# First gemm of the FFNs: products V and W2 accumulate onto the banks of X and W

## The chip, the cores and the metric

The kernel runs on one core of a Trainium2 chip. The metric is device time in microseconds (us) of one execution, taken as the median of three runs. PE is the matmul engine, DVE the vector engine, ACT the activation engine, POOL the GpSimd engine, SP the queue that issues DMAs.

## The reference

Two layers of a diffusion backbone work on 768 tokens (256 context, 512 latent) of width 1024. Each layer is FFN, token mixer, FFN; layer 0 mixes by differential attention, layer 1 by neighbourhood attention. The change is in the FFNs, of which there are four:

```python
def _ffn_sublayer(h, mod, g_pre, g_post, w_in, w_out):
    shift, scale, gate = mod
    u = _modulate(_rmsnorm(h, g_pre), shift, scale)
    a, b = jnp.split(u @ w_in, 2, axis=-1)
    y = (jax.nn.silu(a) * b) @ w_out
    return h + MACARON_W * gate * _rmsnorm(y, g_post)
```

Here `u @ w_in` (1024 by 2 x 2816) is the first gemm. Shift, scale and gate come from another product, of SiLU(c) with a table of adaLN weights.

## The kernel before

The four FFNs are named f00, f01, f10, f11 (layer, then first or second of the layer). Tokens are worked on as two sets of 384, in f11 as two sets of 256. The first gemm (`FirstGemm`) splits its weights into 11 column groups of 256 columns, numbered 0 to 10, once for the gate half (`a`, which goes through SiLU) and once for the other half (`b`, which is multiplied on): items run a0, b0, a1, ... b10, and the trace names what belongs to item a9 of f00 as f00a9. Raw weights and their splits carry the number of the item in the load order instead: f0025 is item a9, f0026 is b9.

Each item is a product of 2 x 2 blocks done by seven block products instead of eight, the scheme of Strassen and Winograd: `X` = A11 with the first set's upper half, `V` = A12 with its lower half, `Y`, `Z`, `W` and `W2` of sums of weight blocks (S1 and S2 in tile `s12`, S3 and S4 in tile `s34`) with sums of the inputs or the second set, `Z2` of block A22. The sums of weights are POOL's (L473 to L476). Each operand is kept as a high and a low part: ACT casts the high part (L126), DVE subtracts to get the low part (L127). In the trace these tiles end in h and l: a1h, a1l for A11 and A12; bh, bl for `s12`; ch, cl for `s34`; dh, dl for A22. One block product is then four slices of the inner dimension times three passes, so 12 matmuls (L132), and within each slice the third pass is the one that reads the low part of the weights.

Items are of two kinds. The kind is set by EARLY = (7, 7, 6, 5): for the first 7, 7, 6, 5 groups of f00, f01, f10, f11 the first two products were done earlier, and X comes back from memory as `p1`; these items (kind R) have five products, 60 matmuls, and the others (kind F) seven, 84 matmuls. So there are 50 R items and 38 F items.

PSUM is held by two pools: `psum_g` has two tiles of one bank, `psum_y` three tiles of two banks. X and Y are the two banks of one `psum_y` tile, Z and W of another; V, Z2 and W2 are tiles of `psum_g`. In the trace, an instruction on Y or W is named after its tile, X or Z.

DVE adds the products together: `u` = X + Y (L548, after ACT copied X at L561), c1 = u + Z, c1's second half = that + W, `u` = u + W, c1 += Z2, c0's second half = u + W2, and in F items c0's first half = V + `u`. Then ACT applies SiLU (a items) or DVE and POOL multiply (b items, L593 and L584), and the result `h` goes to memory. A second gemm reads it back; its first split of `h` (f00hl, f01hl) is made in the DVE queue while the first gemm runs.

Between the products `work.step` issues pieces of other work: in R items, while they last, the adaLN product (`mods_pairs`, tile `am`, L243), a group of four matmuls of 32 x 512 that write the four strips of 32 partitions of one `psum_g` tile, followed by a DVE add (`mb`, L247). There are 24 such groups in f00, 16 in f01, 24 in f10 and none in f11. The same form of matmul stands at the start of the kernel as `md` (L165). The trace has two records for each of these matmuls.

The program is written through a tile framework, which tracks dependencies by whole tile and chooses the order of instructions on each engine itself; the order of the code is only its input.

Of the kernel before, what the change touches and what calls it, by code (L numbers as in the profile page):

```python
# [12 lines left out]
AF = mybir.ActivationFunctionType  # L13
ALU = mybir.AluOpType
# [42 lines left out]
def kernel(  # L57
# [20 lines left out]
    nc = tc.nc  # L78
# [32 lines left out]
    def psum_g(name):  # L111
        return psg.tile([P, 512], F32, tag="g", name=name)

    def psum_y(name):
        return psy.tile([P, 2 * 512], F32, tag="y", name=name)
# [11 lines left out]
        eng.tensor_tensor(out=lo, in0=src, in1=hi.bitcast(F32), op=ALU.subtract)  # L127
        return hi, lo

    def mm3(ps, lhs, rhs, first=True, last=True):  # L130
        for n, (i, j) in enumerate(PASSES):
            nc.tensor.matmul(ps, lhsT=lhs[i], rhs=rhs[j], start=first and n == 0, stop=last and n == 2)  # L132

    svec = const.tile([P, 5 * KC], F32, name="svec")
    nc.sync.dma_start(svec, cvec)
# [231 lines left out]
    class Work:  # L367
# [3 lines left out]
        def add(self, g):  # L371
            self.gens.append(g)
# [45 lines left out]
    class FirstGemm:  # L418
# [82 lines left out]
            self.load(1)  # L501
            self.step(0)

        def prod(self, ps, a, b):
            for k in range(4):
                mm3(ps, [x[:, k, :] for x in a], [x[:, k, :] for x in b], k == 0, k == 3)

        def cols(self, t, k0):
            c = slice(t * P, t * P + self.n)
# [32 lines left out]
        def group(self, i, kind_, g, x, work):  # L542
            n, pool, nm = self.n, self.pool, f"{self.nm}{'ab'[x]}{g}"
            o = self.ops[i]
            S = [[y[:, q] for y in o[s]] for s in ("S12", "S34") for q in (0, 1)]
            T = [[y[:, q] for y in self.sums["T"]] for q in range(3)]
            nx = lambda m=1: self.step(i + 1, m)
            add = lambda out, a, b: nc.vector.tensor_tensor(out=out, in0=a, in1=b, op=ALU.add)  # L548
            if x == 0:
                self.sa = pool.tile([P, 2, 2 * n], F32, tag="sa", name=nm + "sa")  # L550
            sa = self.sa
            c = [sa[:, y, :] if x == 0 else pool.tile([P, 2 * n], F32, tag=f"c{y}", name=f"{nm}c{y}") for y in range(2)]
            u2 = pool.tile([P, n], F32, tag="u2", name=nm + "u")
            nx()
            XY = psum_y(nm + "X")
            X, Y = XY[:, 0:n], XY[:, 512 : 512 + n]
            if kind_ == "F":
                self.prod(X, [y[:, 0:4] for y in o["A1"]], self.cols(self.t1, 0))
            self.prod(Y, S[1], T[1])
            if kind_ == "F":  # L560
                nc.scalar.copy(u2, X)  # L561
                V = psum_g(nm + "V")[:, 0:n]
                self.prod(V, [y[:, 4:8] for y in o["A1"]], self.cols(self.t1, 4))
                add(c[0][:, 0:n], V, u2)
                add(u2, Y, u2)
            else:
                add(u2, Y, o["p1"])
            nx()
            ZW = psum_y(nm + "Z")
            Z, W = ZW[:, 0:n], ZW[:, 512 : 512 + n]  # L570
            self.prod(Z, S[2], T[2])
            self.prod(W, S[0], T[0])
            add(c[1][:, 0:n], u2, Z)
            add(c[1][:, n:], c[1][:, 0:n], W)
            add(u2, u2, W)
            nx()
            work.step(1)
            Z = psum_g(nm + "Z2")[:, 0:n]
            self.prod(Z, o["A22"], self.cols(self.t2, 0))
            add(c[1][:, 0:n], c[1][:, 0:n], Z)  # L580
            if x == 0:
                nc.scalar.activation(c[1], c[1], AF.Silu)
            else:
                nc.gpsimd.tensor_tensor(out=sa[:, 1, :], in0=sa[:, 1, :], in1=c[1], op=ALU.mult)  # L584
            W = psum_g(nm + "W2")[:, 0:n]
            self.prod(W, S[3], self.cols(self.t2, 4))
            nx(9)
            add(c[0][:, n:], u2, W)
            f0 = n if kind_ == "R" else 0
            if x == 0:  # L590
                nc.scalar.activation(sa[:, 0, f0:], c[0][:, f0:], AF.Silu)
            else:
                nc.vector.tensor_tensor(out=sa[:, 0, f0:], in0=sa[:, 0, f0:], in1=c[0][:, f0:], op=ALU.mult)  # L593
                c0 = self.t1 * P
                nc.sync.dma_start(hdr[self.slot][2 * g][:, c0 + f0 : c0 + 2 * n], sa[:, 0, f0:])
                nc.sync.dma_start(hdr[self.slot][2 * g + 1][:, c0 : c0 + 2 * n], sa[:, 1, :])
            work.step(1)
# [143 lines left out]
    def out_ahead(l, w_out, sets, done):  # L741
# [25 lines left out]
        for hf in range(2):  # L767
            c = slice(hf * 512, hf * 512 + 512)
            ws = [split(r[:, :, c], [P, 2, 512], f"{nm}w{hf}{q}") for q, r in enumerate(raws)]
            for i in range(len(tiles)):  # L770
                ps = psum_g(f"{nm}g{hf}{i}")
                for u in range(HELD):
                    w = [x[:, u % 2] for x in ws[u // 2]]
                    mm3(ps, [o[:, x, u, i * P : (i + 1) * P] for x in range(2)], w, u == 0, u == HELD - 1)
                    if u == HELD // 2 - 1:
                        yield 9
                nc.scalar.copy(part[:, i, c], ps)
                yield 9

    def outproj(pool, l, w_out, sets, nxt, more, ahead):  # L780
# [49 lines left out]
        def mm(ps, q, i, c, first, last):  # L830
            hh, w = ops[q]
            mm3(ps, [x[:, i * P : (i + 1) * P] for x in hh], [x[:, c] for x in w], first, last)
# [151 lines left out]
    def attend(nslot, qk, vs, scores, values, rate, pattern, prog, ahead, opening):  # L984
        def stream():
            v = iter(())
            for u in range(1, 8):
# [3 lines left out]
                for x in pattern:  # L991
                    src = v if x == "V" else g
                    if next(src, "end") != "end":
# [18 lines left out]

        first = {"q": qk(0, "q"), "k": qk(0, "k"), "V": vs(0)}
        for x in opening:
# [383 lines left out]
    with Main("m0") as mp:  # L1398
        first = FirstGemm(mp, 0, 0, full, "f00", lead=True)
# [16 lines left out]
        for x in SCRIPT.split():  # L1416
            if x[0] == "m":
                hf, m, n = (int(y) for y in x[1:])
# [116 lines left out]
```

## Time and profile before

| | |
|---|---|
| median of three runs | 2891.31 us (2886.37 to 2895.78) |
| the profiled execution | 2882.43 us, of which the span is 2880.0 us |
| mean granted PE clock | 0.988 |
| PE busy | 2755.4 us, 96% of the span, 15928 records |
| DVE busy | 1986.4 us, 69% |
| ACT, POOL busy | 1209.5 us (42%), 883.0 us (31%) |

The span is from the first to the last instruction of the profiled execution. Busy shares are means over stages of different kind, so each stage has to be read by itself.

### The profile page before, as it was taken

The page shows a single profiled execution, that of the slowest core. Times are in us where ns is not written, and L with a number is a line of the kernel's source. Part 1 is how long each engine was busy: PE and PEld are TensorE (multiplying, and loading weights), DVE is VectorE, ACT ScalarE, POOL GpSimd, SP SyncE. Part 2 cuts the span into 40 slices and gives each one's busy share as a digit, 9 for nine tenths or more (in the row PEclk, how much of TensorE's full clock was granted, in tenths as well). Part 3 has the DMA queues.
Part 4 walks back from the last instruction along what each step waited for, and adds up shares of the span by engine and source line. Part 5 has one row for each costly group of instructions (what it writes and reads, how often), then busy time and mean ns, then how long its engine had stood idle before and what let it go on. Part 6 is the DMA issues. An engine that isn't in the chain of part 4 may idle for free. (4 is left out here: it accounts for less than half of the span.)

```text
span 2880.0 us, 41455 instructions
## 1 busy us (share of the span) xinstructions
PE 2755.4 (96%) x15928; PEld 2441.6 (85%) x15928; DVE 1986.4 (69%) x2554; ACT 1209.5 (42%) x1894; POOL 883.0 (31%) x715
## 2 busy tenths in 40 slices
PE   7799999999999988999999999999999999889999
PEld 5788998888888778899988888998878888789987
DVE  5677664667777696777555867674654556799965
ACT  5322333435555553233343522233444446544444
POOL 2455420020000055554210455340122110377710
PEclk9999999999999999999999999999999999999999
DMA  8577346643343476853465577436644444654375
GB/s 279 189 278 273 103 147 218 213 123 86 105 118 88 140 240 199 285 172 104 171 210 193 178 271 266 162 107 219 217 160 118 118 118 130 222 167 147 125 252 192
DMA packets 304820, 511.55 MB, mean 178 GB/s; under 512 B 17456, under 2 KB 226224, under 8 KB 297456
## 3 DMA queue, kind: packets, MB, share of 16 engines
q1 hardware_dynamic: 304336, 508.26, 53.7%
q8 instruction: 125, 2.05, 0.3%
q14 instruction: 71, 0.58, 0.1%
q10 hardware_dynamic: 288, 0.66, 0.1%
HBM read 410.15 MB, written 63.05 MB: 164 GB/s over the span
## 5 line engine op out<-in xcount | busy, mean ns | idle before, releaser
L1243 POOL TENSOR_TENSOR bias<-bp,nneg 128x128 f32<-128x128 f32 x112 | 52.3, 505 | 190.1 <-issue 99.2
L127 DVE TENSOR_TENSOR f01hl<-f01h,f01hh 128x384 fp32r<-128x384 f32 x44 | 26.4, 599 | 74.7 <-ACT f01hh L126 74.6
L127 DVE TENSOR_TENSOR f00hl<-f00h,f00hh 128x384 fp32r<-128x384 f32 x44 | 26.5, 602 | 72.9 <-ACT f00hh L126 72.8
L127 DVE TENSOR_TENSOR f10hl<-f10h,f10hh 128x384 fp32r<-128x384 f32 x44 | 26.0, 591 | 67.7 <-ACT f10hh L126 67.6
L243 PE MATMUL am<-aw,s 128*32 128x512 f32 x512 | 68.3, 606 | 4.1 <-DVE f10b0c L548 3.0
L126 ACT CAST f10hh<-f10h 128x384 fp32r<-128x384 f32 x44 | 22.7, 516 | 113.6 <-PE f10y L721 93.9
L126 ACT CAST f01hh<-f01h 128x384 fp32r<-128x384 f32 x44 | 22.7, 516 | 109.8 <-PE f01y L721 95.1
L126 ACT CAST f00hh<-f00h 128x384 fp32r<-128x384 f32 x44 | 22.7, 516 | 107.2 <-PE f00y L721 92.7
L132 PE MATMUL av<-pt,davh 128*128 128x256 f32 x224 | 44.6, 292 | 0.0
L247 DVE TENSOR_TENSOR mb<-am,mb 128x512 f32<-128x512 f32 x64 | 43.7, 683 | 0.0
L1305 PE MATMUL nav<-npt,navh 128*64 128x256 f32 (+1 forms) x320 | 39.3, 365 | 0.0
L132 PEld LDWEIGHTS av<-pt,davh 128*128 128x128 f32 x224 | 36.4, 193 | 1.3 <-ACT pt L1165 0.2
L1305 PEld LDWEIGHTS nav<-npt,navh 128*64 128x64 f32 x320 | 22.0, 136 | 12.2 <-issue 1.9
L132 PE MATMUL av<-pt,davl 128*128 128x256 f32 x112 | 31.7, 283 | 0.0
L126 ACT CAST f11hh<-f11h 128x256 fp32r<-128x256 f32 x44 | 17.7, 406 | 33.1 <-DMA f11h<-hr 22.1
L127 DVE TENSOR_TENSOR f11hl<-f11h,f11hh 128x256 fp32r<-128x256 f32 x44 | 20.2, 464 | 13.4 <-ACT f11hh L126 13.4
L243 PEld LDWEIGHTS am<-aw,s 128*32 128x32 f32 x512 | 10.1, 108 | 20.4 <-issue 10.2
L282 POOL TENSOR_SCALAR f01y0r<-f01y0s 128x1 f32<-128x1 f32 x1 | 0.2, 192 | 84.5 <-ACT f01y0j L276 84.5
L282 POOL TENSOR_SCALAR f10y0r<-f10y0s 128x1 f32<-128x1 f32 x1 | 0.2, 192 | 84.5 <-ACT f10y0j L276 84.5
L282 POOL TENSOR_SCALAR f00y0r<-f00y0s 128x1 f32<-128x1 f32 x1 | 0.2, 192 | 84.5 <-ACT f00y0j L276 84.5
L282 POOL TENSOR_SCALAR f00y3r<-f00y3s 128x1 f32<-128x1 f32 x1 | 0.2, 193 | 79.3 <-ACT f00y3j L276 79.3
L282 POOL TENSOR_SCALAR f10y3r<-f10y3s 128x1 f32<-128x1 f32 x1 | 0.2, 192 | 79.3 <-ACT f10y3j L276 79.3
(9736 smaller groups left out, 11615.4 us busy)
## 6 DMA issues: line engine op xcount, KB each, us to landing
aw<-in_ada_w SPq DMA_DIRECT2D x63, 1024.0 KB
f00r<-in_ffn_w_in SPq DMA_DIRECT2D x22, 1024.0 KB
f01r<-in_ffn_w_in SPq DMA_DIRECT2D x22, 1024.0 KB
f10r<-in_ffn_w_in SPq DMA_DIRECT2D x22, 1024.0 KB
f11r<-in_ffn_w_in SPq DMA_DIRECT2D x22, 1024.0 KB
f00o<-in_ffn_w_out SPq DMA_DIRECT2D x21, 1024.0 KB
f01o<-in_ffn_w_out SPq DMA_DIRECT2D x21, 1024.0 KB
f10o<-in_ffn_w_out SPq DMA_DIRECT2D x21, 1024.0 KB
```

The source lines that it names most:

```text
L126: nc.scalar.copy(hi, src)
L127: eng.tensor_tensor(out=lo, in0=src, in1=hi.bitcast(F32), op=ALU.subtract)
L132: nc.tensor.matmul(ps, lhsT=lhs[i], rhs=rhs[j], start=first and n == 0, stop=last and n == 2)
L243: nc.tensor.matmul(ps[32 * c : 32 * c + 32], lhsT=s32[:, k], rhs=w[:, c // 2, c % 2 * 512 : c % 2 * 512 + 512], start=True, stop=True,)
L247: nc.vector.tensor_tensor(out=acc, in0=ps, in1=acc, op=ALU.add)
L282: nc.gpsimd.tensor_scalar(r, ss, 1.0, EPS, ALU.mult, ALU.add)
L1243: nc.gpsimd.tensor_tensor(out=bias[:, m, :].rearrange("p (a b) -> p a b", a=8), in0=view, in1=neg[:, m, :].rearrange("p (a b) -> p a b", a ...
L1305: nc.tensor.matmul(av[64 * i : 64 * i + 64, half * 256 + c0 : half * 256 + c0 + n], lhsT=made[u]["v"][0][:, key, vc : vc + 64], rhs=made[u ...
```

## The change

V is no longer a tile of its own. Once the copy of X has been taken, V's twelve matmuls accumulate onto X's bank (no start flag), so that the bank holds X + V, and SiLU (a items) or a new DVE multiply (`times`, b items) reads it from there. W2 accumulates likewise onto W's bank, after W has been added to c1, and the add of W to `u` goes away. The add c1 = Z + u moves in the code to between products Z and W. The copy of X moves to right behind X, and V to behind W. The multiply of the first row of halves is two instructions of 384 columns for an F item, where it was one of 768. So one DVE add goes from each R item and two from each F item; the count of matmuls stays. `skip_group_check` relaxes a check in the simulator and is no instruction.

```diff
@@ -127,9 +127,11 @@
         eng.tensor_tensor(out=lo, in0=src, in1=hi.bitcast(F32), op=ALU.subtract)
         return hi, lo
 
-    def mm3(ps, lhs, rhs, first=True, last=True):
+    def mm3(ps, lhs, rhs, first=True, last=True, onto=False):
         for n, (i, j) in enumerate(PASSES):
-            nc.tensor.matmul(ps, lhsT=lhs[i], rhs=rhs[j], start=first and n == 0, stop=last and n == 2)
+            nc.tensor.matmul(
+                ps, lhsT=lhs[i], rhs=rhs[j], start=first and n == 0, stop=last and n == 2, skip_group_check=onto
+            )
 
     svec = const.tile([P, 5 * KC], F32, name="svec")
     nc.sync.dma_start(svec, cvec)
@@ -501,9 +503,9 @@
             self.load(1)
             self.step(0)
 
-        def prod(self, ps, a, b):
+        def prod(self, ps, a, b, onto=False):
             for k in range(4):
-                mm3(ps, [x[:, k, :] for x in a], [x[:, k, :] for x in b], k == 0, k == 3)
+                mm3(ps, [x[:, k, :] for x in a], [x[:, k, :] for x in b], k == 0 and not onto, k == 3, onto)
 
         def cols(self, t, k0):
             c = slice(t * P, t * P + self.n)
@@ -551,46 +553,45 @@
             sa = self.sa
             c = [sa[:, y, :] if x == 0 else pool.tile([P, 2 * n], F32, tag=f"c{y}", name=f"{nm}c{y}") for y in range(2)]
             u2 = pool.tile([P, n], F32, tag="u2", name=nm + "u")
+            times = lambda out, y: nc.vector.tensor_tensor(out=out, in0=y, in1=out, op=ALU.mult)
             nx()
             XY = psum_y(nm + "X")
             X, Y = XY[:, 0:n], XY[:, 512 : 512 + n]
             if kind_ == "F":
                 self.prod(X, [y[:, 0:4] for y in o["A1"]], self.cols(self.t1, 0))
+                nc.scalar.copy(u2, X)
             self.prod(Y, S[1], T[1])
-            if kind_ == "F":
-                nc.scalar.copy(u2, X)
-                V = psum_g(nm + "V")[:, 0:n]
-                self.prod(V, [y[:, 4:8] for y in o["A1"]], self.cols(self.t1, 4))
-                add(c[0][:, 0:n], V, u2)
-                add(u2, Y, u2)
-            else:
-                add(u2, Y, o["p1"])
+            add(u2, Y, u2 if kind_ == "F" else o["p1"])
             nx()
             ZW = psum_y(nm + "Z")
             Z, W = ZW[:, 0:n], ZW[:, 512 : 512 + n]
             self.prod(Z, S[2], T[2])
+            add(c[1][:, 0:n], Z, u2)
             self.prod(W, S[0], T[0])
-            add(c[1][:, 0:n], u2, Z)
-            add(c[1][:, n:], c[1][:, 0:n], W)
-            add(u2, u2, W)
+            add(c[1][:, n:], W, c[1][:, 0:n])
+            if kind_ == "F":
+                self.prod(X, [y[:, 4:8] for y in o["A1"]], self.cols(self.t1, 4), True)
+                if x == 0:
+                    nc.scalar.activation(sa[:, 0, 0:n], X, AF.Silu)
+                else:
+                    times(sa[:, 0, 0:n], X)
             nx()
             work.step(1)
             Z = psum_g(nm + "Z2")[:, 0:n]
             self.prod(Z, o["A22"], self.cols(self.t2, 0))
-            add(c[1][:, 0:n], c[1][:, 0:n], Z)
+            add(c[1][:, 0:n], Z, c[1][:, 0:n])
             if x == 0:
                 nc.scalar.activation(c[1], c[1], AF.Silu)
             else:
                 nc.gpsimd.tensor_tensor(out=sa[:, 1, :], in0=sa[:, 1, :], in1=c[1], op=ALU.mult)
-            W = psum_g(nm + "W2")[:, 0:n]
-            self.prod(W, S[3], self.cols(self.t2, 4))
+            self.prod(W, S[3], self.cols(self.t2, 4), True)
             nx(9)
-            add(c[0][:, n:], u2, W)
-            f0 = n if kind_ == "R" else 0
+            add(c[0][:, n:], W, u2)
             if x == 0:
-                nc.scalar.activation(sa[:, 0, f0:], c[0][:, f0:], AF.Silu)
+                nc.scalar.activation(sa[:, 0, n:], c[0][:, n:], AF.Silu)
             else:
-                nc.vector.tensor_tensor(out=sa[:, 0, f0:], in0=sa[:, 0, f0:], in1=c[0][:, f0:], op=ALU.mult)
+                times(sa[:, 0, n:], c[0][:, n:])
+                f0 = n if kind_ == "R" else 0
                 c0 = self.t1 * P
                 nc.sync.dma_start(hdr[self.slot][2 * g][:, c0 + f0 : c0 + 2 * n], sa[:, 0, f0:])
                 nc.sync.dma_start(hdr[self.slot][2 * g + 1][:, c0 : c0 + 2 * n], sa[:, 1, :])
```

Line numbers behind this point are two higher after the change (L243 becomes L245, L247 becomes L249, L548 becomes L550); `times` is L556.

In the built program the order of instructions changes with it. On PE, at item a5 of f00 (kind R), before: the end of product Z (weights f0017c), product W (weights f0017b) and the adaLN group behind it.

```order
L132 MATMUL f00a5Z_2198<-inTh_454,f0017cl_2155 128x384
L132 MATMUL f00a5Z_2198<-inTh_454,f0017bh_2114 128x384
L132 MATMUL f00a5Z_2198<-inTl_455,f0017bh_2114 128x384
...
L132 MATMUL f00a5Z_2198<-inTh_454,f0017bl_2115 128x384
L243 MATMUL am060_2230<-aw060_2051,s32_179 32x512 [waits DMAHW4_49,DVE_49]
L243 MATMUL am060_2230<-aw060_2051,s32_179 32x512 x3
L132 MATMUL f00a5Z2_2238<-inuh_196,f0017dh_2158 128x384 [waits DVE_49,Activation_49]
```

The same place after:

```order
L132 MATMUL f00a5Z_2178<-inTh_454,f0017cl_2135 128x384
L245 MATMUL am060_2209<-aw060_2033,s32_179 32x512 [waits DMAHW4_49,PE_49]
L132 MATMUL f00a5Z_2178<-inTh_454,f0017bh_2095 128x384 [waits DVE_49]
L132 MATMUL f00a5Z_2178<-inTl_455,f0017bh_2095 128x384
...
L132 MATMUL f00a5Z_2178<-inTh_454,f0017bl_2096 128x384
L245 MATMUL am060_2209<-aw060_2033,s32_179 32x512 x3
L132 MATMUL f00a5Z2_2217<-inuh_196,f0017dh_2138 128x384 [waits Activation_49]
```

The first matmul of W has a wait on DVE that it did not have, for the add of Z (c1 = Z + u), since Z and W are one tile. One matmul of the adaLN group has moved ahead of W, the other three have stayed behind it. This split of a group stands in 30 items: 12 in f00 (b0, a1, b1, a2, and both of groups 3 to 6), 8 in f01 (the same as far as b4), 10 in f10 (the same as far as b5).

On PE, at the start of item a9 of f00 (kind F), before: X, Y and V of twelve each, and then Z, with its first use of the low part of `s34`.

```order
L132 MATMUL f00a9V_3171<-inuh_196,f0025a1l_3060 128x384
L132 MATMUL f00a9Z_3190<-inTh_454,f0025ch_3123 128x384 [waits Activation_49]
L132 MATMUL f00a9Z_3190<-inTl_455,f0025ch_3123 128x384
L132 MATMUL f00a9Z_3190<-inTh_454,f0025cl_3124 128x384 [waits DVE_49]
```

After, the same matmuls stand right behind X, ahead of Y:

```order
L132 MATMUL f00a9X_3105<-inuh_196,f0025a1l_3009 128x384
L132 MATMUL f00a9Z_3136<-inTh_454,f0025ch_3083 128x384 [waits DVE_49,Activation_49]
L132 MATMUL f00a9Z_3136<-inTl_455,f0025ch_3083 128x384
L132 MATMUL f00a9Z2_3180<-inuh_196,f0025dh_3087 128x384
L132 MATMUL f00a9Z_3136<-inTh_454,f0025cl_3084 128x384 [waits DVE_49]
L132 MATMUL f00a9X_3105<-inTh_454,f0025bh_3052 128x384 [waits Activation_49]
```

The matmul that needs f0025cl was the 39th of the item and is the 16th. Behind it come Y (12), the rest of Z, five matmuls of V, W (12, its first one waiting for DVE), the other seven of V, Z2 and W2. A b item has four of Z there and nothing of Z2. In f11's F items two (a) or four (b) matmuls of Z2 and all of Y come between Z's second and third.

On DVE, the end of item b8 of f00 (f00b8; f0025 is the next item, a9), before:

```order
L127 TENSOR_TENSOR f0025bl_3092<-f0025s12_3012,f0025bh_3091 128x1024 [waits Activation_49]
L548 TENSOR_TENSOR f00b8c1_3010<-f00b8c1_3010,f00b8Z2_3095 128x384 [waits DVE_49,PE_49]
L127 TENSOR_TENSOR f0025dl_3128<-f00r25_2882,f0025dh_3127 128x512 [waits Activation_49]
L548 TENSOR_TENSOR f00b8c0_3009<-f00b8u_3011,f00b8W2_3110 128x384 [waits DVE_49,PE_49]
L593 TENSOR_TENSOR f00a8sa_2884<-f00a8sa_2884,f00b8c0_3009 128x768 [waits DVE_49]
L127 TENSOR_TENSOR f0025cl_3124<-f0025s34_3013,f0025ch_3123 128x1024 [waits Activation_49]
```

and after, from the adds of the item on:

```order
L550 TENSOR_TENSOR f00b8u_2974<-f00b8X_2981,f00b8u_2974 128x384 [waits PE_49,Activation_49]
L550 TENSOR_TENSOR f00b8c1_2973<-f00b8Z_3012,f00b8u_2974 128x384 [waits DVE_49,PE_49]
L550 TENSOR_TENSOR f00b8c1_2973<-f00b8Z_3012,f00b8c1_2973 128x384 [waits DVE_49,PE_49]
L127 TENSOR_TENSOR f0025a1l_3009<-f00r25_2848,f0025a1h_3008 128x1024 [waits DMAHW2_49,Activation_49]
...
L550 TENSOR_TENSOR f00b8c1_2973<-f00b8Z2_3056,f00b8c1_2973 128x384 [waits DVE_49,PE_49]
L127 TENSOR_TENSOR f0025dl_3088<-f00r25_2848,f0025dh_3087 128x512 [waits Activation_49]
L550 TENSOR_TENSOR f00b8c0_2972<-f00b8Z_3012,f00b8u_2974 128x384 [waits PE_49]
L556 TENSOR_TENSOR f00a8sa_2850<-f00b8c0_2972,f00a8sa_2850 128x384 [waits DVE_49]
L127 TENSOR_TENSOR f0025cl_3084<-f0025s34_2976,f0025ch_3083 128x1024 [waits Activation_49]
```

The subtraction that makes the next item's f0025cl has stayed the last of the item, behind the add of W2 and the multiply. The adds of Z and of W stand one right behind the other, and nothing of the splits stands between them; this holds in R items too.

## Rows read from the trace of the kernel before

**Rows 1.** Busy time by window: length, PE, PEld, DVE, ACT, POOL, clock, DMA share, GB/s.

```profile
147.60:296.20 148.60, 148.60 (x880) 125.73 (x877) 110.26 (x139) 39.59 (x49) 75.42 (x52) 1.00 0.79 278
296.20:416.50 120.30, 120.30 (x697) 119.12 (x696) 84.04 (x97) 41.21 (x49) 49.26 (x33) 1.00 0.28 96
...
2554.10:2672.00 117.90, 108.03 (x873) 106.39 (x872) 114.72 (x135) 49.36 (x65) 90.25 (x57) 0.99 0.46 151
2672.70:2755.00 82.30, 82.30 (x682) 82.00 (x681) 76.14 (x94) 38.36 (x48) 56.35 (x33) 1.00 0.39 130
```

**Rows 2.** PE's waits in the first gemms: total, times, longest.

```profile
PE f00b0W L132 <- DVE mb L247: 2.2, 1, 2.2
PE f01b0W L132 <- DVE mb L247: 5.1, 1, 5.1
...
PE f11b4Z L132 <- DVE f1114cl L127: 1.7, 1, 1.7
```

**Rows 3.** Timeline of item b5 of f00 (R), PE, then DVE: start, duration.

```profile
263.06 0.33 PE L132 MATMUL f00b5Z<-inTh,f0018ch 128*128 128x384 f32 x1
...
265.14 0.33 PE L132 MATMUL f00b5Z<-inTh,f0018bh 128*128 128x384 f32 x1
...
267.31 1.06 PE L243 MATMUL am<-aw,s 128*32 128x512 f32 x8
268.31 0.45 PE L132 MATMUL f00b5Z<-inuh,f0018dh 128*128 128x384 f32 x1
268.59 0.34 PE L132 MATMUL f00b5Z<-inul,f0018dh 128*128 128x384 f32 x1
...
263.25 0.56 DVE L548 TENSOR_TENSOR f00b5u<-f00b5X,f0018p 128x384 f32<-128x384 f32 x1 [0.52 <-PE f00b5X L132]
...
269.54 1.22 DVE L127 TENSOR_TENSOR f0019cl<-f0019s,f0019ch 128x1024 fp32r<-128x1024 f32 x1
```

**Rows 4.** Timeline of PE at the kernel's start, where `md` stands.

```profile
9.12 1.93 PE L165 MATMUL md<-aw,s 128*32 128x512 f32 x8 [0.68 <-DMA aw<-in_ada_w]
...
19.95 1.92 PE L165 MATMUL md<-aw,s 128*32 128x512 f32 x2
21.80 1.97 PE L201 MATMUL in2T<-ident,un 128*128 128x128 f32 x8
23.70 2.07 PE L165 MATMUL md<-aw,s 128*32 128x512 f32 x14
```

**Rows 5.** Timeline of f00's F items b8 to b9: PE, DVE, POOL.

```profile
357.78 0.33 PE L132 MATMUL f00a9X<-inuh,f0025a1h 128*128 128x384 f32 x1
...
364.02 0.33 PE L132 MATMUL f00a9Z<-inTh,f0025ch 128*128 128x384 f32 x1
...
372.34 0.33 PE L132 MATMUL f00b9X<-inuh,f0026a1h 128*128 128x384 f32 x1
...
358.45 0.54 DVE L548 TENSOR_TENSOR f00b8c<-f00b8u,f00b8W 128x384 f32<-128x384 f32 x1
359.02 2.03 DVE L593 TENSOR_TENSOR f00a8sa<-f00a8sa,f00b8c 128x768 f32<-128x768 f32 x1
360.98 2.31 DVE L127 TENSOR_TENSOR f0025cl<-f0025s,f0025ch 128x1024 fp32r<-128x1024 f32 x1
...
373.53 1.81 DVE L127 TENSOR_TENSOR f0026cl<-f0026s,f0026ch 128x1024 fp32r<-128x1024 f32 x1
...
360.20 2.00 POOL L474 TENSOR_TENSOR f0026s<-f0026s,f00r 128x512 f32<-128x512 f32 x1
```

**Rows 6.** Timeline of f11 (R item a3 to b3), DVE, then PE.

```profile
2605.13 0.42 DVE L548 TENSOR_TENSOR f11a3sa<-f11a3u,f11a3Z 128x256 f32<-128x256 f32 x1
...
2606.25 2.05 DVE L127 TENSOR_TENSOR f1112cl<-f1112s,f1112ch 128x1024 fp32r<-128x1024 f32 x1
...
2608.36 0.39 PE L132 MATMUL f11b3Z<-o1Th,f1112cl 128*128 128x256 f32 x1 [1.75 <-DVE f1112cl L127]
```

**Rows 7.** Timeline of DVE in item b0 of f01 (R).

```profile
1146.71 0.56 DVE L127 TENSOR_TENSOR f01hl<-f01h,f01hh 128x384 fp32r<-128x384 f32 x1 [8.71 <-ACT f01hh L126]
```

## The prediction

> **What bounds the kernel now.** The table of windows comes first, because a mean over the kernel hides what differs here [rows 1]. Its first two rows are f00's first gemm, R items and then F items. PE is busy for the whole length of both (148.60 of 148.60, 120.30 of 120.30) while DVE has a third of its time free (84.04 of 120.30 in the F items). So in f00 nothing that DVE is spared can come back on the path: PE's matmuls are the path, and their number stays. The third and fourth rows are f11, first mostly R items, then F items. In the third, DVE has 114.72 of 117.90 us and PE only 108.03: there DVE sets the pace. The list of PE's waits says the same [rows 2]: the first gemms hold two waits at W2 of an item b0 (2.2 and 5.1 us) and, in f11, waits of Z for the low part of `s34`, the longest 1.7 us. What the change can gain is thus small, and is known: two waits of 7.3 us together, and DVE's time in ten items of f11. The question is what the new order costs where PE had no gap at all.
>
> From the window rows I take the pace of a matmul: 120.30 us over 697 gives 0.173 us for 384 columns, 82.30 over 682 gives 0.121 for 256 [rows 1]. A block product of twelve is then 2.08 us, in f11 1.45 us.
>
> How long PE must wait when DVE stands between two of its matmuls comes from three rows. Product Y of f00b5 ends where Z begins, at 263.06, and the add on it starts at 263.25 [rows 3]: 0.2 us. The add takes 0.55. In f11 a subtraction ends at 2606.25 + 2.05 = 2608.30 and the matmul that waited for it starts at 2608.36 [rows 6]: 0.06 us. From the end of product Z to a W that waits for the add of Z it is therefore 0.2 + 0.55 + 0.06 = 0.8 us, if DVE is free.
>
> **The change part by part.**
>
> *First, the split adaLN group, in 30 R items.* W now waits 0.8 us for the add of Z, and the scheduler has put one of the four `am` matmuls into that gap. What does a lone one cost? The trace has such a case among the `md` matmuls, which have the same form [rows 4]: two records (one matmul) at 19.95 take 1.92 us, and the next matmul starts 1.85 us later; eight records (four matmuls) at 9.12 take 1.93. There a lone one costs as much as four. Fourteen records at 23.70 take 2.07, about two groups at the 1.06 us that a full one takes in f00b5 [rows 3], so three cost as much as four as well. The one at 19.95 was at half pace, where the product at 9.12 was too; at full pace I take half of 1.85, 0.92 us. Leaving the 128-column matmuls and coming back costs something besides: behind `am` the first matmul of Z2 takes 268.59 - 268.31 = 0.28 instead of 0.17 [rows 3], so 0.1, and I take as much at the entry, 0.2 in all. The three that stay behind W cost what the group cost before. So an item grows by 0.92 + 0.2 = 1.1 us, and the 0.8 us wait is hidden in it: 30 x 1.1 = 33 us. Bounds: if a lone one cost a quarter of a group, the item would still stand through the wait of 0.8, and the three left would save 0.25, so 0.55 net, 16 us; at most a whole group with its switch, 1.06 + 0.2, 38 us.
>
> The Trainium skill, page "TensorEngine Tiling (Array Packing)", section "Key Properties", says that different tiles can execute in parallel and that a change of tiling mode drains TensorE; by it a lone strip runs as long as four and each of the two extra changes costs a drain that the page does not price, so the sum would be the 33 us or more. The row at 19.95 agrees with the first half.
>
> *Second, the early use of `s34`'s low part, in the F items of f00, f01, f10.* A9 shows it [rows 5]. Its X starts at 357.78, and its Z at 364.02. The subtraction f0025cl is the last of DVE's queue in item b8; it starts at 360.98 and ends at 363.29, 5.5 us behind X's start, and 0.7 us ahead of Z. That was in time. After the change the matmul that needs it is the 16th of the item: 15 x 0.173 = 2.6 us behind X's start. DVE still has to add W2 (which ends only where X starts), multiply, and then subtract. The add may start at 358.45 as now, 0.7 us behind X's start, and takes 0.54; the multiply is 384 columns wide instead of 768, about half of 2.03; the subtraction takes 2.31: 0.7 + 0.54 + 1.0 + 2.31 = 4.6, some 4.7 us with the gaps. PE would wait 4.7 - 2.6 = 2.1 us at every start of an a item. At a b item the multiply is missing and the subtraction took 1.81: in the trace f0026cl ends at 375.34, 3.0 us behind b9X's start at 372.34, and is needed at 14 x 0.173 = 2.4 us: 0.6 us, or 0.2 where DVE is ahead; I take 0.35. A pair costs 2.45 us, and the three gemms have 4 + 4 + 5 = 13 pairs: 32 us, of which I take 2 off for the entry from R items, where PE still has `am` to do. So 30 us. Bounds: low, every operation at its quickest and the add at once, 0.2 + 0.55 + 0.55 + 1.81 = 3.1 us, 0.5 per pair, 7 us; high, the subtraction ends as late as it does now, 5.5, so 2.9 + 0.6 per pair, 45 us.
>
> What the 2.31 rests on: POOL multiplied and added beside that subtraction (its add at 360.20 took 2.00), and with POOL quiet the same shape takes 1.22 [rows 3, 5]. The Trainium skill, "GPSIMD Engine Reference", section "Key points", says that POOL shares its SBUF interfaces with VectorE and contends with instructions of two SBUF inputs. By it, if the new order put POOL's work elsewhere, a pair would save 1.1 us and the sum 14; but POOL's multiply still follows the same add, so I keep 2.31.
>
> *Third, b0 of f00 and f01.* The queue of DVE holds there the first split of the second gemm's `h`, and this waits for a transfer: f01hl starts at 1146.71 after 8.71 us of idle time [rows 7]. The add of Z stands behind it. Before, only W2 had to wait for what follows; now W waits already, one product (2.08 us) and an `am` group (1.06) earlier. 3 us each, 6 us in sum (0 to 9).
>
> *Fourth, the ten R items of f00, f01, f10 without `am`.* Five to seven matmuls of Z2 fill the wait (5 x 0.173 = 0.87 against 0.8), so 0.2 each, 2 us.
>
> *Fifth, f11's ten R items,* where DVE sets the pace. It is spared one add, 0.42. But the adds of Z and of W are now a fixed pair: the add of Z ends, W starts 0.06 later, runs 1.45, and its add starts 0.2 behind it. DVE stands still for 1.7 us in that gap, where before it went on at once, from 2605.13 through the adds to the subtraction at 2606.25 [rows 6]. Part of this was slack behind PE's own waits, and DVE with less to do beside POOL is quicker; I take +0.6 of the 1.3 net, 6 us (-4, the spared add alone, to +15).
>
> *Sixth, f11's F items.* DVE has 76.14 us of 82.30, which is 18.7 us in a pair of items of 2 x 84 x 0.121 = 20.3. Spared are four adds, 1.7 us; forced idle time is 2 x 1.7 = 3.4. That makes 20.4 without any other wait, and up to 22.5 with the waits that DVE has for Y and Z2. So 0.1 to 4 a pair; I take 2.2, and 13 us for six pairs (1 to 25).
>
> *At nothing:* the copy of X ahead of Y is hidden by Z's matmuls (4 x 0.173 = 0.7), V behind the add of Y by the rest of Z, W2 by V's last seven and Z2; without that cover each costs 0.8. The `psum_g` tiles that come free are worth something only in the two b0 items.
>
> Sum: 33 + 30 + 6 + 2 + 6 + 13 = 90 us. Against the profiled execution, 2882.43, this gives 2972. That one lies 8.9 below the median of the runs shown, so for the median I forecast 2891.31 + 90, rounded to 2980.
>
> **The rivals.**
>
> *Half.* F items' DVE keeps up (bound of the second part, 7 us) and f11 costs nothing, for DVE has 36 us to spare in f00's F window; what remains is 33 + 7 + 6 = 46, 2936. Against it: the queue is in order, and 0.5 us a pair needs every operation at its quickest at once.
>
> *Worse.* The waits add up, since a late DVE is late for the next item too: 38 for the adaLN groups, 45, 9, 15 and 25 are 132, 3023. For it: f11's DVE has no reserve. Against it: f00 has.
>
> *No change.* The filling matmuls do their work: a lone `am` overlaps with W, and the adds come in time. It needs 0 from parts one and two together, below both bounds; within 9 us, 2891. For it stands that 0.87 us of Z2 covers the wait of 0.8 in the items without `am`. The Trainium skill, "TensorE: Matmul & The Clock Gate", Part 2, says that matmuls stay in program order and only weight loads are pulled ahead; by it a waiting W holds up all behind it. The 1.75 us wait of f11b3 held PE as a whole and agrees [rows 6].
>
> *Faster.* f11's DVE decides: it is spared 0.42 in each of ten R items and 1.7 in each of six F pairs, and the b0 waits of 7.3 us go with the `psum_g` tiles that are no longer asked for. At most 4 + 7 us of this lies on the path, 2880. It decides if DVE's gap between the two adds is filled or the waits stay under 0.2 us an item.
>
> **How the numbers follow.** Forecast (60 to 120 above) 0.60, half 0.18, worse 0.12, no change 0.06, faster 0.04. A measurement can tell 0.3%, 8.7 us, from no change. The range leaves out the last two and the end of worse: 2930 to 3025. Faster 0.04, same 0.06, slower 0.90.
>
> **What the profile after would show.** Right: in f00's R items an `am` row of two records, some 0.9 us, ahead of each W, with no wait of W behind it; in F items of f00 a wait of Z for the low part of `s34`, 2 us at a items and under 0.6 at b items, so that the F window's PE falls from 100% to 92%; a wait of W in b0 of f01 beyond 5.1. In f11, DVE idle for 1.7 us between the adds of Z and W. Wrong: `am` rows of two records under 0.4 us, F windows still at 100%, or an f11 that is shorter than before.

## The result

The changed kernel takes 3013.28 us (median of four runs, 3010.33 to 3016.3); the kernel before, timed with it, 2890.12. The ratio is 1.0424, 95% interval 1.0404 to 1.0445: slower, by 123 us. The forecast was 2980 in a range of 2930 to 3025.

The profiled execution of the changed kernel has a span of 3010.6 us, 130.6 more than before. Its first part, which answers to the busy times in the table above:

```profile
PE 2829.6 (94%) x15928; PEld 2464.2 (82%) x15928; DVE 1916.5 (64%) x2447; ACT 1205.0 (40%) x1913; POOL 872.9 (29%) x715
```

PE has the same 15928 records and is busy 74 us longer; DVE has 107 instructions fewer and is spared 70 us. The rest of the loss, 56 us, is PE standing still. What DVE was spared shows as a gain in none of the stretches below.

Where it went is read from the time at which each item starts on PE in the two traces. The table gives, for each stretch, its length before and the growth in the changed kernel; "b0" runs from the start of a0 to that of a1, "R" from there to the second F item, "F" from there to the second gemm. In f10 the kernel before starts its second F item, b6, with four matmuls that stand ahead of W2 and an `am` group of a6; these 3.17 us are counted to R, as they are after the change.

```
stretch            f00            f01            f10            f11
b0           25.6  +6.1     30.5  +2.5     29.5 +13.4     22.3  +4.0
R           166.5 +15.5    156.7 +17.0    149.4  +5.6     81.1  +6.9
F           101.9 +13.6    101.9 +12.2    133.6 +11.7    110.9 +16.9
all else: +5.3
```

Before rounding these sum to the 130.6. In the R items of f00, two groups of rows show the split of the adaLN group. This is PE at item b5, the place of [rows 3]:

```profile
282.55 0.34 PE L132 MATMUL f00b5Z<-inTh,f0018cl 128*128 128x384 f32 x1
282.82 1.04 PE L245 MATMUL am<-aw,s 128*32 128x512 f32 x2
283.80 0.45 PE L132 MATMUL f00b5Z<-inTh,f0018bh 128*128 128x384 f32 x1
284.08 0.34 PE L132 MATMUL f00b5Z<-inTl,f0018bh 128*128 128x384 f32 x1
...
286.11 1.06 PE L245 MATMUL am<-aw,s 128*32 128x512 f32 x6
```

The lone matmul (two records) takes 1.04 us, the other three (six records) 1.06, as much as four did before. W has no wait behind it: its add had come. The group of all `am` rows shows the sum of it, 99.4 us where it was 68.3 (before, then after; behind the second bar stands how long PE stood idle just before them, and for whom):

```profile
L243 PE MATMUL am<-aw,s 128*32 128x512 f32 x512 | 68.3, 606 | 4.1 <-DVE f10b0c L548 3.0
L245 PE MATMUL am<-aw,s 128*32 128x512 f32 x512 | 99.4, 605 | 0.0
```

In the F items, PE and DVE at the start of a9 of f00, the place of [rows 5]:

```profile
386.69 0.34 PE L132 MATMUL f00a9Z<-inuh,f0025dh 128*128 128x384 f32 x1
389.23 0.44 PE L132 MATMUL f00a9Z<-inTh,f0025cl 128*128 128x384 f32 x1 [2.19 <-DVE f0025cl L127]
...
389.69 0.51 PE L132 MATMUL f00a9X<-inTl,f0025bh 128*128 128x384 f32 x1
389.99 0.52 PE L132 MATMUL f00a9X<-inTh,f0025bl 128*128 128x384 f32 x1
...
392.87 0.45 PE L132 MATMUL f00a9X<-inTh,f0025bl 128*128 128x384 f32 x1
393.15 0.34 PE L132 MATMUL f00a9Z<-inTh,f0025ch 128*128 128x384 f32 x1
...
384.77 0.55 DVE L550 TENSOR_TENSOR f00b8c<-f00b8Z,f00b8u 128x384 f32<-128x384 f32 x1
385.35 1.62 DVE L556 TENSOR_TENSOR f00a8sa<-f00b8c,f00a8sa 128x384 f32<-128x384 f32 x1
386.89 2.28 DVE L127 TENSOR_TENSOR f0025cl<-f0025s,f0025ch 128x1024 fp32r<-128x1024 f32 x1
```

X starts at 384.27 and the subtraction ends at 389.17, 4.9 us later. PE waits 2.19 us. Then the matmuls come 0.30 to 0.32 us apart instead of 0.173, up to 393.15: the granted clock is 0.50 there, the lower of its two levels (1.2 of 2.4 GHz), for most of Y. The windows of three a items, with the granted clock third from the end, show that this does not always follow (the first row is the stretch of Y just named):

```profile
389.70:393.10 3.40, 3.40 (x12) 3.40 (x11) 0.00 (x0) 0.00 (x0) 2.06 (x2) 0.50 0.51 204
384.27:402.92 18.65, 16.45 (x85) 16.04 (x85) 10.58 (x11) 5.50 (x7) 7.71 (x7) 0.91 0.29 99
...
1965.48:1982.56 17.08, 14.89 (x86) 14.47 (x85) 10.59 (x11) 5.50 (x7) 7.73 (x7) 1.00 0.32 109
...
2029.62:2048.25 18.63, 16.44 (x85) 16.02 (x85) 10.05 (x11) 5.50 (x7) 6.33 (x5) 0.91 0.28 99
```

The items are a9 of f00, then a8 and a10 of f10. All three wait 2.2 us; in a8 of f10 the granted clock stays 1.00 and the item is 1.57 us shorter.

At b0 of f10, ACT, DVE and PE:

```profile
1755.85 0.51 ACT L126 CAST f10hh<-f10h 128x384 fp32r<-128x384 f32 x1 [16.94 <-DMA f10h<-hr]
...
1741.19 0.56 DVE L550 TENSOR_TENSOR f10b0c<-f10b0Z,f10b0u 128x384 f32<-128x384 f32 x1 [0.60 <-PE f10b0Z L132]
1756.39 0.56 DVE L127 TENSOR_TENSOR f10hl<-f10h,f10hh 128x384 fp32r<-128x384 f32 x1 [14.65 <-ACT f10hh L126]
1756.87 0.55 DVE L550 TENSOR_TENSOR f10b0c<-f10b0Z,f10b0c 128x384 f32<-128x384 f32 x1
...
1757.47 0.69 PE L132 MATMUL f10b0Z<-f01uh,f107ch 128*128 128x384 f32 x1 [9.74 <-DVE f10b0c L550]
```

The split of h (f10hl) stands between the add of Z and the add of W, and waits 14.65 us for the cast of h, which waits for its transfer. That no split stands between the two adds, as said with the change, thus does not hold here, nor at b1 of f11. W2 accumulates onto W and so waits for the add of W: 9.74 us.

In f11's F items DVE has the gap between the two adds (a8), 1.88 us:

```profile
2820.65 0.42 DVE L550 TENSOR_TENSOR f11a8sa<-f11a8Z,f11a8u 128x256 f32<-128x256 f32 x1
2822.96 0.42 DVE L550 TENSOR_TENSOR f11a8sa<-f11a8Z,f11a8sa 128x256 f32<-128x256 f32 x1 [1.88 <-PE f11a8Z L132]
```

### The profile page after: what moved, and what is told of

The parts are those of the page before. It is cut to its first block, busy times and chain, and to the rows that moved or that the text cites. A ratio compares the mean times of both kernels' runs of the same rounds, so it can differ in the third digit from the quotient of the medians.

```text
span 3010.6 us, 41390 instructions
## 1 busy us (share of the span) xinstructions
PE 2829.6 (94%) x15928; PEld 2464.2 (82%) x15928; DVE 1916.5 (64%) x2447; ACT 1205.0 (40%) x1913; POOL 872.9 (29%) x715
## 5 line engine op out<-in xcount | busy, mean ns | idle before, releaser
L245 PE MATMUL am<-aw,s 128*32 128x512 f32 x512 | 99.4, 605 | 0.0
L249 DVE TENSOR_TENSOR mb<-am,mb 128x512 f32<-128x512 f32 x64 | 43.9, 686 | 13.1 <-PE am L245 13.1
L245 PEld LDWEIGHTS am<-aw,s 128*32 128x32 f32 x512 | 14.0, 108 | 23.8 <-issue 21.3
L1306 PEld LDWEIGHTS nav<-npt,navh 128*64 128x64 f32 x320 | 22.0, 136 | 12.2 <-issue 1.9
```

Source lines behind the costliest of these rows:

```text
L245: nc.tensor.matmul(ps[32 * c : 32 * c + 32], lhsT=s32[:, k], rhs=w[:, c // 2, c % 2 * 512 : c % 2 * 512 + 512], start=True, stop=True,)
L249: nc.vector.tensor_tensor(out=acc, in0=ps, in1=acc, op=ALU.add)
L1306: nc.tensor.matmul(av[64 * i : 64 * i + 64, half * 256 + c0 : half * 256 + c0 + n], lhsT=made[u]["v"][0][:, key, vc : vc + 64], rhs=made[u ...
```

## The experiments

My theory was that two places in the order of the code cost the time, the add of Z ahead of W and the copy of X ahead of Y. The rival was the accumulation onto a bank that has just been read.

**Taking the order back, one edit at a time.** The first kernel puts the add behind W again:

```diff
-            add(c[1][:, 0:n], Z, u2)
             self.prod(W, S[0], T[0])
+            add(c[1][:, 0:n], Z, u2)
```

> The changed kernel, but the add c1 = Z + u stands behind product W again, as before the change; V and W2 still accumulate, and the copy of X still stands ahead of Y. Theory: the loss has two causes in the order of the code, the add of Z ahead of W (W waits for DVE, so the adaLN group is split) and the copy of X ahead of Y (Z is drawn forward in F items). Here the first is gone: no adaLN group is split in the built program, R items are as long as before (36 us back), the waits at b0 shrink (8 us back), and F items keep their wait of 2.2 us for the low part of s34 and the slow matmuls behind it. 2945 us, 2930 to 2960. Rival, the accumulation onto a bank that has just been read costs the time itself: within 10 us of the changed kernel, 3003 to 3015.

2934.1 us, ratio to the kernel before 1.0152 (1.0137 to 1.0167): 79 us came back. Growth in R of f00 is 0.4 us instead of 15.5, at b0 of f10 nothing instead of 13.4; F of f00 and f01 still lose 9.1 and 9.3.

The second puts the copy behind Y again:

```diff
-                nc.scalar.copy(u2, X)
             self.prod(Y, S[1], T[1])
+            if kind_ == "F":
+                nc.scalar.copy(u2, X)
```

> The changed kernel, but the copy of X stands behind product Y again; the add of Z stays ahead of W, V and W2 accumulate. Theory: in the built program Z stands behind X and Y again (its third matmul is the 27th of an F item, 4.5 us behind X's start, and the low part of s34 comes at 4.9), so F items of f00, f01, f10 lose 0.4 us a pair instead of 3 to 4.5, with no drop of the clock: 35 us back there and some 8 in f11's F items. The split adaLN groups stay, 1.2 us in each of 30 R items. 2970 us, 2955 to 2985. Rival, accumulation costs: no more than 10 us back, over 3000.

2975.61 us, 1.0297 (1.0282 to 1.0313): 38 us came back. F of f00, f01 and f10 grow by 2.2, 2.2 and 3.3 us, where it was 13.6, 12.2 and 11.7. The wait at an a item of f00 is now 0.3 us:

```profile
PE f00a9Z L132 <- DVE f0025cl L127: 0.3, 1, 0.3
```

f11's F items, where I had expected 8 us back, gave 1.5. The gap of DVE is still there, but that it is what they lose to is not shown: the next kernel has no such gap and loses more in them.

Both edits together leave only the accumulations and the spared adds of the change:

> The changed kernel with both the add of Z behind W and the copy of X behind Y, as before the change: the two accumulations and the spared DVE adds alone. Theory: nearly all of the 123 us is gone; F items have Z at 4.5 us against the low part at 4.9 or so, 5 us in sum; f11's R items gain from the spared add: 2892 us, 2880 to 2905. Rival, the accumulation itself costs half or more of the loss: 2950 or more.

2908.19 us, 1.0063 (1.0048 to 1.0078), 3 us above what I had written. Of the 123 us 105 are gone; the rival is out. What is left lies in f11's F items (+18.1), where every a item waits for the low part. V behind W draws Z forward by one product, which fits, but was not undone by itself:

```profile
PE f11a8Z L132 <- DVE f1121cl L127: 2.0, 1, 2.0
```

**One edit put into the kernel before.** The add of Z alone, ahead of W:

```diff
-            self.prod(W, S[0], T[0])
             add(c[1][:, 0:n], u2, Z)
+            self.prod(W, S[0], T[0])
```

> The kernel before, with one edit: the add c1 = Z + u ahead of product W. Nothing accumulates, no add is spared. Theory: adaLN groups are split in 30 R items, 1.2 us each, 36 us; b0 items wait for the split of h, 13 us; f11's DVE gets its gap between the adds, 10 to 15 us; F items of f00, f01, f10 nothing, for six matmuls of Z2 fill the wait. 2950 us, 2935 to 2965. Rival, accumulation costs: under 2905.

2976.38 us, 1.0299 (1.0282 to 1.0316): 86 us, 26 more than I had summed. R items grow by 1.20 us with a group and 0.07 without, as forecast. Too small were b0 (24 us, three split groups among them, where I had 13; f10's W2 waits 11.4) and f11 (23): there W waits for the add of Z, since DVE gets to it late. At the F items of f00, f01 and f10, where I had expected nothing, an a item lost 1.0 us (3.3, 3.3 and 4.4 us in sum).

```profile
PE f10b0W L132 <- DVE mb L247: 11.4, 1, 11.4
...
PE f11a8Z L132 <- DVE f11a8sa L548: 1.5, 1, 1.5
```

W2 alone, accumulating onto W:

```diff
-            add(u2, u2, W)
...
-            W = psum_g(nm + "W2")[:, 0:n]
-            self.prod(W, S[3], self.cols(self.t2, 4))
+            self.prod(W, S[3], self.cols(self.t2, 4), True)
```

> The kernel before with one edit: W2 accumulates onto W's bank, so the add of W to u is gone (one DVE add of 0.55 us less in each of 88 items); V, the copy of X and the other adds stay as before. The order of PE is that of before. Theory: the accumulation costs nothing by itself, since W2 stands a whole product behind the add of W; it gains only where DVE sets the pace, in f11's R items, 1 to 3 us. What took the both_back kernel to 2908 was V behind W, which draws Z forward in F items. 2889 us, 2880 to 2898. Rival, accumulating onto a bank just read costs: 2905 or more.

2890.8 us beside 2888.42, ratio 1.0007 (0.9998 to 1.0016). 88 accumulations onto a bank that DVE read one product earlier, and 88 spared adds, change nothing that can be measured. f11's R items are 4.7 us shorter in the trace, its F items 5.6 longer, so only the sum is nothing there.

**What the lone adaLN matmul costs, apart from the wait.** Both groups of an item behind W2:

```diff
-            work.step(1)
             Z = psum_g(nm + "Z2")[:, 0:n]
...
-            work.step(1)
+            work.step(2)
```

> The changed kernel, but both adaLN groups of an R item are issued behind W2 (one call of two steps in place of two calls). W still waits for the add of Z, and in the built program five matmuls of Z2 fill that wait, with no group split. Theory: the loss in R items is the lone adaLN matmul and not the wait, so all of it goes: 1.2 us in 30 items, 36 us, and 0.2 more where one change of shape is spared; F items and f11 as in the changed kernel. 2973 us, 2960 to 2985. Rival, the wait for DVE is the loss and would stand anyway: 3000 or more.

3006.64 us, 1.0413 (1.0396 to 1.043): a miss, on the rival's side, but for a cause that neither had named. Groups that stand one behind the other wait for weights, 13.6 us in sum:

```profile
PE am L245 <- DMA aw<-in_ada_w: 13.6, 8, 4.0
```

What else kept the time from coming back I have not followed. So this kernel does not tell the two apart. The same edit in the kernel with W2 alone was made in the hope of sparing a change of shape:

> The kernel before with W2 accumulating onto W (as in w2_only), and both adaLN groups of an R item issued together behind W2. Theory: one change between the shapes of matmul is spared in 32 R items, 0.2 us each, 6 us in sum, and the b0 items lose up to 3 of it. 2886 us, 2876 to 2896, faster than the kernel before by about what can be measured. Rival, two groups in a row wait for each other's bank or for their weights: 2900 or more.

2902.85 us, 1.0049 (1.0036 to 1.0061), slower, with eleven such waits, 15.4 us in sum. The kernel that does tell them apart has the first group behind Z2:

```diff
-            work.step(1)
             Z = psum_g(nm + "Z2")[:, 0:n]
             self.prod(Z, o["A22"], self.cols(self.t2, 0))
+            work.step(1)
```

> The changed kernel, but the first adaLN group of an R item is issued behind product Z2 instead of ahead of it; the two groups of an item are not neighbours, as they were in groups_last, where the second one waited for its weights. W still waits for the add of Z; in the built program five matmuls of Z2 fill that wait and no group is split. Theory: items of the changed kernel without a group grew by 0.05 us, those with a split group by 1.20, so 30 x 1.15 = 34 us come back, less what DVE is late for the add of Z: 2980 us, 2970 to 2990. Rival, the wait for DVE costs it whatever fills it: 3003 or more.

2984.57 us, 1.0324 (1.0308 to 1.034): 29 us came back, as forecast. PE at b3 of f00, with Z2, then W, and no wait:

```profile
221.79 0.34 PE L132 MATMUL f00b3Z<-inul,f0014dh 128*128 128x384 f32 x1
221.97 0.39 PE L132 MATMUL f00b3Z<-inTh,f0014bh 128*128 128x384 f32 x1
222.19 0.33 PE L132 MATMUL f00b3Z<-inTl,f0014bh 128*128 128x384 f32 x1
```

Most R items of f00 now grow by 0.05 us instead of 1.20. W's wait is covered by five matmuls of Z2 at no price; the price was that of the matmul that had been put there.

**How late the low part may be.** The second half's multiply goes from DVE to POOL:

```diff
-                times(sa[:, 0, n:], c[0][:, n:])
+                nc.gpsimd.tensor_tensor(out=sa[:, 0, n:], in0=c[0][:, n:], in1=sa[:, 0, n:], op=ALU.mult)
```

> The changed kernel, but the multiply of the second half in b items is POOL's instead of DVE's, so that the next item's low part of s34 comes 1 to 1.6 us earlier. Theory: the F items of f00, f01, f10 lose 4.5 us a pair because that low part is late by 2.2 us and because PE's clock falls behind most of these waits; with a wait of 1.1 us or less the clock stays up and a pair loses 1.5 to 2: 30 us back, and some 6 in f11. 2977 us, 2960 to 2990. Rival, the order of PE itself (Z drawn ahead of Y, V in two pieces) costs the time and the low part does not: 3005 or more.

2975.03 us, 1.0299 (1.0285 to 1.0313). The wait at f00's a items is 0.8 us, and F of f00, f01, f10 grow by 4.4, 4.5 and 4.9 us. A pair loses 1.4 in f00 where it lost 4.5. The second row is item a9 of f00, with a granted clock of 1.00:

```profile
PE f00a9Z L132 <- DVE f0025cl L127: 0.8, 1, 0.8
...
382.71:398.45 15.74, 14.92 (x86) 14.50 (x86) 9.15 (x10) 5.50 (x7) 9.52 (x8) 1.00 0.34 118
```

A wait shortened by 1.4 us gave back 3.1 a pair in f00, since the clock stays up as well.

**The split of h at b0.** It goes to POOL, in the kernel before and in the changed one:

```diff
-            split(hraw[q][:, 0:n], None, "", [y[:, 0:n] for y in hh])
+            split(hraw[q][:, 0:n], None, "", [y[:, 0:n] for y in hh], nc.gpsimd if q == 0 else nc.vector)
```

> The kernel before, with the low part of the second gemm's first slice of h made by POOL instead of DVE (its cast stays with ACT). This split waits for a transfer, and in item b0 DVE's queue stands behind it. Theory: W2's waits at b0 of f00 and f01 (2.2 and 5.1 us) and that of the adaLN group at a1 of f10 (3.0) go, up to 10 us; ACT's queue still stands behind the cast, so part of it may come back one item later: 2882 us, 2875 to 2889. Rival, POOL's sums of weights, which stand behind the split now, are late in place of DVE's adds: 2889 or more.

2888.25 us beside 2889.81, ratio 0.9994 (0.9985 to 1.0003). f00 and f01 gain 1.5 and 4.3 us at b0 and lose 1.5 and 1.7 in the R items behind it, f10 loses 5.3 there: no gain that can be measured.

> The changed kernel with the same move of the first split of h to POOL. Theory: the b0 items lose 18 us to that split (5 in f00, 1 in f01, 12 in f10, where the add of W stands behind it and W2 waits for that add), because the adds of Z and W may not pass it in DVE's queue; with it gone 12 to 18 us come back and the rest of the loss stays: 2998 us, 2990 to 3005. Rival, the loss at b0 comes from ACT's queue, which stands behind the same transfer: no more than 5 us back, 3008 or more.

3001.66 us, 1.0387 (1.0373 to 1.0402): 12 us came back, at the edge of what I had written. At the b0 items of f00, f01 and f10 28 us went, but f10's R items grew by 12.5 more, all in a1. PE waits there for ACT, whose queue stands behind the cast of h, and then for DVE (0.6 and 3.0 us):

```profile
PE f10a1Z L132 <- ACT f108ch L126: 4.2, 1, 4.2
```

**Whether the two losses add.** The copy behind Y and the first group behind Z2, both edits shown above:

> The changed kernel with two edits that gave time back one at a time: the copy of X behind product Y (2975.6 us alone) and the first adaLN group behind Z2 (2984.6 alone). Theory: the two losses lie in different items (F and R) and add, 37.7 + 28.7 us back from 3013.3: 2947 us, 2938 to 2956. What is left then is the split of h at b0 (some 20 us), f11, where DVE stands between the adds of Z and W (some 25), and the rest of R. Rival, the two share a cause (a late DVE), and the second gives back less than half: 2960 or more.

2946.67 us, 1.0195 (1.0178 to 1.0212), where the sum was 2947. The losses of F and R items are two, and they add.

## Why the prediction was right, and where its sizes were off

The sign, the two main places and the range held; the size was 33 us too small. The likeliest case had 60 to 120 us, and 123 lies a little beyond it, towards the rival "worse" (132). Term by term, against the 130 us between the two profiled executions:

*Split groups, forecast 33.* 30 items at 1.20 make 36. The lone matmul took 1.04, read from an `md` row at half pace. The kernel with the group behind Z2 shows that this term is the lone matmul's and not the wait's.

*Early use of the low part, forecast 30.* F from the second F item on grew by 37.5. The wait of 2.1 us at an a item came as 2.19, the subtraction at 4.9 us as forecast 4.7. The step said nothing of what PE does after the wait: in six of the nine a items of these stretches the clock fell and the item took 1.57 us more, 9 us in sum; without these 9 the term is 28. The other three lost 2.5. The b items lost 0.2 to 0.4, as said. The subtraction beside POOL came as assumed, 2.28 us for 2.31. The Trainium skill ("GPSIMD Engine Reference", "Key points") says that POOL shares its SBUF interfaces with VectorE and contends with its instructions of two SBUF inputs. The trace agrees: in a9 of f00 POOL's sum ran beside the first 1.2 us of the subtraction; at the entry to b8, where it ended 0.35 us after the subtraction had begun, the same shape took 1.43.

*b0, forecast 6.* This step failed in its size. The b0 items lost 22 us, 18.4 without their split groups. Of that, f00 and f01 lost 4.9 and 1.3, where each was given 3: the sum came out by luck. The other 12 are f10's, which the step left out. It asked only whether W waits behind the split of h. In f10 the split stands one place later, between the two adds, and W2 now waits for the second of them, which it had not before. The kernel before paid for the same transfer one item later, at a1, with 6.3 us; the page has 3.0 of them, the wait of the `am` row above, which the prediction's list of waits left out. So f10's net loss there is about 6.

*R items without a group, forecast 2.* R of f00, f01 and f10 grew by 38.1 us, less 27 x 1.2 = 32.4, so 5.7, or 12 without the 6.3 us that a1 of f10 no longer pays. Most of these items took 0.05 each, but in a5 and a6 of f01, as in a5 of f00, W waited 1.4 to 1.7 us for the add of Z. At a5 that add is late behind two `mb` multiplies (L257, L259) of 1.8 and 2.2 us and a split, at a6 behind a split of 2.87. In f01 the first F item, a7, is in this stretch too, with 4.6.

*f11, forecast 6 and 13.* 10.8 and 16.9. The gap of DVE between the adds came as forecast (1.7; 1.88 in a8). Put into the kernel before, the add of Z alone cost f11's F items 14.2; yet with both edits taken back, and no gap, they lose 18.1. How the 16.9 divides between the gap and the early Z stays open. The upper bound of 4 us a pair had no working: its own rows go up to 2.2, and the pairs from a6 on lost 3.3 each.

Not priced at all: 5 us outside the first gemms, which I have not followed.

The rival "half" fails on the F items, "no change" on both main terms, "faster" on f11. That the accumulation itself is free was taken for granted in the prediction, since only waits were priced; the kernel with W2 alone shows it for W2. For V it was not measured by itself, only together with its place behind W.

No version beat the kernel before by what can be measured.

## What to carry to other kernels

When two products share a tile, an add on one half is a wait for the other: look in the built order for what the scheduler puts into that wait, and price the filler, for it can cost more than the wait. When an edit moves a product forward, ask which operand it now needs first, and where that operand stands in the queue of the engine that makes it. A DVE add removed where PE is busy throughout is worth nothing: 88 removed adds by themselves changed the time by nothing that can be measured.

## What the runs showed of the hardware

A pause of PE of 2.2 us was followed in six F items of nine (a8 to a10 of three gemms) by matmuls at little more than half pace over some 3.6 us, at a granted clock of 0.91 for the item against 1.00 in the three others; what sets these apart stays open. After a wait of 0.8 us in the same place, in the kernel with POOL's multiply, the granted clock was 1.00 in the F items of these gemms, and a pair lost 1.4 us in f00. One matmul of 32 columns of weights took 1.04 us where four side by side took 1.06.
